# A first stage in a new order: norm rows spread by TensorE, low weight halves last, v statistics on ACT

## The chip, the cores and the metric

The kernel runs on one core of a Trainium2 chip. The metric is the device time of one execution in microseconds (us). It is 938.45 as the median of three runs of the kernel before (935.6 to 940.73).

## The reference, cut to what matters

One layer of a decoder trunk on 512 tokens of 1024 channels, in float32. The change touches the front of it: the first norm, the branch that computes v and u from the normed x, and the gating of the two.

```
x = layer_norm(x, ln_in_g, ln_in_b)                     # 512 x 1024
z = x @ w_in + b_in                                     # split into u_a, v_a, x_b, gate_b, q_c, merge
v = layer_norm(gelu(v_a), ln_v_g, ln_v_b)               # 512 x 1024
s = einsum('gts,bcsgd->bctgd', tril(w_s), v as chunks of 128 x 8 groups of 128) + b_s
o_a = gelu(u_a) * s                                     # branch A
...                                                     # branch B (recurrence), branch C (attention)
y = g_a * (o_a @ p_a) + g_b * (o_b @ p_b) + g_c * (o_c @ p_c)
x = layer_norm(ALPHA * x + y @ w_o + b_o, ...);  x = layer_norm(ALPHA * x + moe(x), ...)
```

## The kernel before, in words

All products of the trunk are made of three float32r products: each operand is split into a high part (a cast on ACT, line 82) and a low part (a subtraction on DVE, line 83), and TensorE adds hi x hi, hi x lo and lo x hi into one PSUM bank. `split` (lines 81 to 83) makes the two halves, `mm3` (lines 107 to 109) the three products.

The stages follow each other on TensorE: the v products, the u loop with the mixing of v (branch A), the merge of branch A with its gates, the attention branch with its merge, the recurrent branch with its gates, the output projection and the router, then sixteen experts in 18 blocks of tokens, and the last norm.

**The v stage** (lines 270 to 373) stands in a manual block: inside it every engine gets the instructions in the order in which they are written. x lies in four blocks of 128 tokens. For each block it takes the norm (statistics by two bn_stats, a reciprocal root by eight steps on one column, `rstd_ops`, then a centring and a scaling over 1024 columns), the transposes (`transx`, eight of 128x128 into two PSUM banks, each bank then split by two casts and two subtractions) and two products p(t, n) of 24 matmuls each, one for each half n of the 1024 v columns. Weights come as four raw tiles of 1 MB, two for each n. `split_w` makes both halves of a half tile at once. In `vmm` a product takes, for each half of the channels, hi x hi, lo x hi and hi x lo in turn. `vsplit` puts the transposes of the next block of x after the first eight matmuls of a product. `vout` adds the bias on DVE and takes the gelu on ACT, `vnorm` takes the statistics and the norm of v on DVE.

The two rows ln_in_g and ln_in_b come as DMAs that spread one row over 128 partitions (`bcast`, 512 KB each), issued on SP's queue behind the first block of x and ahead of the weights.

**Outside the manual block** a planner sets the order. It may put instructions of later code among those of the manual block where an engine has room: `residual` (lines 317 to 320, ALPHA x plus b_o, stored by POOL for later) and a chain on 10 columns for the recurrence (lines 539 to 554, with one exp on ACT) are written behind the block and run inside its time. The u loop (lines 384 to 406) is planned too: for each of eight groups g a product of 24 matmuls (`ztile`) gives u, eight short matmuls mix v with the lower triangle of w_s, two DVE steps gate them (lines 400 to 404), and a split writes the result. Each pair of groups has its own weights (`zunit`: a load into one of two raw buffers, two casts, two subtractions). The weights of the pairs after the first are issued only after the last norm of v (lines 385 to 388).

```
for d2 in range(4):
    with ExitStack() as after:
        for i in last if d2 else ():
            after.enter_context(tc.issue_after(i.ins))
        w = zunit(256)
    for c in range(2):
        ...
    residual(d2)
```

PSUM has eight banks: four for products (`mmps`) and four for transposes and the rest (`auxps`). SBUF tiles come from pools with a fixed number of buffers; a new tile waits for the last reader of the buffer that it takes over.

## Time and profile before

| | us |
|---|---|
| median of three runs | 938.45 |
| the profiled execution's own time | 938.02 |
| its span, first to last instruction | 936.3 |
| TensorE busy in it | 875.4 |
| DVE busy | 599.3 |
| ACT busy | 449.2 |
| mean granted TensorE clock | 0.983 |

The span is what the profiler saw of one execution; the execution's own time is a little longer. Every time in the rows further down counts from the start of that span. A busy TensorE is an engine with a matmul in flight, not one at its peak. In the timeline, the bracket behind a row is how long the engine stood idle before it and what ended the wait. The granted clock is 1.00 for 2.4 GHz and 0.50 for 1.2 GHz.

### The profile page before, as it was taken

Reading aid. Unit: us, or ns where it says so; the run is one execution under the profiler, and the core shown is the slowest. Engines: PE = TensorE matmul, PEld = TensorE weight load, DVE = VectorE, ACT = ScalarE, POOL = GpSimd, SP = SyncE. Lnnn points to the kernel's source line nnn. Section 1 sums busy time; section 2 is a strip of 40 time slices with the busy share of each in tenths; the row PEclk is TensorE's granted clock in tenths of the full one; section 3 lists DMA queues with packets and bytes.
Section 4 is the critical chain, followed back from the end, with each engine's and each line's share of the span. In section 5 each row is a group of like instructions: output and inputs, shape, how many; then the busy total and the mean of one; then the engine's idle time right before and its main releaser. Section 6 shows DMA issues by size and latency. Waiting matters only on the chain. (4 is left out here: it accounts for less than half of the span.)

```text
span 936.3 us, 11182 instructions
## 1 busy us (share of the span) xinstructions
PE 875.4 (93%) x4260; PEld 728.6 (78%) x4260; DVE 599.3 (64%) x1020; ACT 449.2 (48%) x628; POOL 90.5 (10%) x86
## 2 busy tenths in 40 slices
PE   3799999999999999999999999999987889999990
PEld 3587888889988888888878888788866778888870
DVE  6978555225555543345766865765288987689966
ACT  4324332224533442224777687533024666678851
POOL 0110000000000100000000000000001123232943
PEclk9999999999999999999999999999999999999995
DMA  8534222223233522212313322338573888799672
GB/s 339 203 113 157 91 90 90 90 90 135 91 97 128 184 90 90 90 57 102 99 69 124 135 74 84 94 121 345 231 275 116 285 308 288 234 311 388 175 170 102
DMA packets 29867, 148.89 MB, mean 159 GB/s; under 512 B 5537, under 2 KB 5793, under 8 KB 16496
## 3 DMA queue, kind: packets, MB, share of 16 engines
q1 hardware_dynamic: 21312, 128.81, 37.7%
q0 software_dynamic: 7056, 17.12, 7.0%
q10 hardware_dynamic: 1440, 2.19, 0.7%
q8 instruction: 35, 0.57, 0.2%
q14 instruction: 24, 0.20, 0.1%
HBM read 138.33 MB, written 18.35 MB: 167 GB/s over the span
## 5 line engine op out<-in xcount | busy, mean ns | idle before, releaser
L109 PE MATMUL mm<-hl 128*128 128x512 f32 x1440 | 333.8, 390 | 0.0
L109 PEld LDWEIGHTS mm<-hl 128*128 128x128 f32 x1440 | 269.1, 188 | 55.6 <-DVE lnr L126 0.2
L83 DVE TENSOR_TENSOR hl<-raw,hl 128x1024 fp32r<-128x1024 f32 (+1 forms) x121 | 142.4, 1183 | 135.4 <-ACT hl L82 134.9
L82 ACT CAST hl<-raw 128x1024 fp32r<-128x1024 f32 (+1 forms) x121 | 121.6, 1016 | 130.2 <-PE mm L109 118.1
L109 PE MATMUL mm<-o,hl 128*128 128x512 f32 x624 | 142.9, 389 | 1.1 <-ACT o L82 1.1
L109 PEld LDWEIGHTS mm<-o,hl 128*128 128x128 f32 x624 | 117.1, 188 | 25.8 <-ACT o L82 1.5
L109 PE MATMUL mm<-hl,xs 128*128 128x512 f32 x432 | 107.5, 404 | 1.1 <-DVE xs L83 1.1
L109 PEld LDWEIGHTS mm<-hl,xs 128*128 128x128 f32 x432 | 81.0, 191 | 20.3 <-DVE xs L83 1.9
L686 DVE TENSOR_TENSOR hl<-o,hl 128x1024 fp32r<-128x1024 f32 (+1 forms) x52 | 57.8, 1144 | 2.6 <-ACT hl L680 2.6
L1137 PE MATMUL mm<-hl,hT 128*128 128x512 f32 x196 | 50.6, 404 | 0.7 <-DVE hT L83 0.7
L680 ACT CAST hl<-o 128x1024 fp32r<-128x1024 f32 x48 | 48.1, 1052 | 1.7 <-PE mm L1137 1.7
L1137 PEld LDWEIGHTS mm<-hl,hT 128*128 128x128 f32 x196 | 35.6, 189 | 8.4 <-DVE hT L83 1.1
L1001 POOL DMA_INDIRECT xg<-x_d,ixg x1 | 1.1, 1092 | 402.3 <-DVE rtl L1060 402.3
L222 ACT ACTIVATE gate<-mm,col 128x512 f32<-128x512 f32 x24 | 16.5, 689 | 39.7 <-PE mm L109 39.6
L1126 DVE TENSOR_TENSOR hl<-raw,hl 128x1024 fp32r<-128x1024 f32 x26 | 30.7, 1223 | 4.5 <-ACT hl L1117 1.9
L1117 ACT CAST hl<-raw 128x1024 fp32r<-128x1024 f32 x32 | 31.9, 1052 | 0.0
L109 PE MATMUL mm<-memT,hl 128*128 128x256 f32 x192 | 27.3, 285 | 0.2 <-ACT memT L82 0.2
L300 PE MATMUL mm<-o,hl 128*128 128x512 f32 x96 | 25.1, 419 | 2.4 <-ACT o L82 2.4
L728 ACT COPY x1T<-aux 128x512 f32<-128x512 f32 x8 | 4.7, 587 | 44.0 <-PE aux L727 19.5
L109 PEld LDWEIGHTS mm<-memT,hl 128*128 128x128 f32 x192 | 24.9, 191 | 0.9 <-ACT memT L82 0.4
L300 PE MATMUL mm<-hl 128*128 128x512 f32 x96 | 25.1, 413 | 0.4 <-DVE hl L83 0.4
L300 PEld LDWEIGHTS mm<-o,hl 128*128 128x128 f32 x96 | 19.2, 204 | 7.3 <-ACT o L82 3.1
(319 smaller groups left out, 1140.9 us busy)
## 6 DMA issues: line engine op xcount, KB each, us to landing
raw<-in_wz_dram SPq DMA_DIRECT2D x32, 1024.0 KB, 4.8
o<-in_we_dram SPq DMA_DIRECT2D x24, 1024.0 KB, 7.4
raw<-in_we_dram SPq DMA_DIRECT2D x16, 1024.0 KB, 5.0
raw<-in_pac_dram SPq DMA_DIRECT2D x8, 1024.0 KB, 4.7
raw<-in_wkv_dram SPq DMA_DIRECT2D x8, 1024.0 KB, 4.9
rawx<-in_we_dram SPq DMA_DIRECT2D x8, 1024.0 KB, 5.9
raw<-in_pb_dram SPq DMA_DIRECT2D x4, 1024.0 KB
raw<-in_wo_dram SPq DMA_DIRECT2D x4, 1024.0 KB, 4.8
```

The lines of the kernel that those rows point to most:

```text
L82: act.copy(hi, src)
L83: dve.tensor_tensor(lo, src, hi.bitcast(F32), op=ALU.subtract)
L109: pe.matmul(ps, lhsT=a(sa_), rhs=b(sb_), start=first and i == 0, stop=last and i == 2)
L222: act.activation(store[j], ps, AF.Sigmoid, bias=cc(C_M + br_i * 8 + j))
L300: pe.matmul(ps, lhsT=xT(k, slice(t * P, (t + 1) * P))(sx), rhs=wv[2 * n + k // 4, k // 2 % 2][:, sw, k % 2, :], start=i == 0, stop=i == 23)
L680: act.copy(t[:, 0], raws[key, i // 2][:, (i % 2) * 1024:(i % 2 + 1) * 1024])
L686: (eng or dve).tensor_tensor(t[:, 1, c0:c1], src[:, c0:c1], t[:, 0, c0:c1].bitcast(F32), op=ALU.subtract)
L728: act.copy(x1T.rearrange("p k n -> p (k n)"), ps)
L1001: pool.indirect_dma_start(out=xg, out_offset=None, in_=x1_d[:, :], in_offset=bass.IndirectOffsetOnAxis(ap=ix[:, b:b + 1], axis=0), bounds_ ...
L1117: act.copy(dnh[key][:, :, n * 512:(n + 1) * 512], dn_half(key, n))
L1126: eng.tensor_tensor(dnl[key][n], dn_half(key, n), dnh[key][:, :, ns].bitcast(F32), op=ALU.subtract)
L1137: pe.matmul(ps, lhsT=hT[:, sa_, f, :], rhs=dn[sb_][:, f, :], start=i + f == 0, stop=i + f == 3)
```

## The change

In the front, all in one manual block that now begins ahead of the first DMA and ends behind the u loop:

- ln_in_g and ln_in_b come as one DMA of two rows (8 KB) into two partitions of the tile that later holds v. TensorE spreads them over 128 partitions with four fp32 matmuls (a column of the identity, repeated, times the rows) into four PSUM banks; two short matmuls on the identity stand ahead of them. x's first block reads its factors from these banks on DVE, and ACT copies them into SBUF for the other blocks.
- A raw weight tile is loaded in two DMAs each. b_s and b_o are loaded last.
- `split_w` becomes `w_hi` (ACT) and `w_lo` (DVE). A product p(t, n) first takes all its 16 hi x hi and lo x hi matmuls, then its 8 hi x lo (`V_KS`). For the first two blocks of x the first 16 of all four products run first, into four open banks, then the last 8 of all four. The low halves of the weights are made in between.
- The sums of x2 and x3 and their squares are taken on ACT (Copy and Square with an accumulator), and one root chain of ten steps serves both. The transposes of x2 and x3 stand ahead of a product and no longer inside one.
- The mean and the variance of v come from the gelu's accumulator and a Square on ACT, and ACT scales v (Identity with scale and bias).
- The two matmuls and eight DVE steps that prepare b_s stand before the last v product, as do the first u weights. The u loop is written out: a product, then the mixing and gating of the group before (`mix_mm` and `mix_ev`, which hold the lines of the old loop), and the residuals in turns 2 to 5.

Elsewhere: the chain on 10 columns is issued after the last exp of the attention; two pad tiles and a wider xb move addresses; the three buffers for gathered tokens are all slices of y (one had its own tile).

```diff
+    const.tile([P, 64], F32, name="pad")
...
+        gi = s0.tile([P, D], F32, name="gi")
+        bi = s0.tile([P, D], F32, name="bi")
+        v = yp.tile([P, NT, AW], F32, name="y")
+        man = ExitStack()
+        man.enter_context(tc.manual_schedule())
+        rw = v[0:2, NT - 1, :]
+        sp.dma_start(rw, rows[0:2, :])
         loadx(0, 2)
-        gi = bcast(sp, s0, "ln_in_g", "gi")
-        bi = bcast(sp, s0, "ln_in_b", "bi")
         raws = [load_w(op_, "o", 2), load_w(hlp, "hl", 2)]
         loadx(1)
-        raws += [load_w(rawp, "raw"), load_w(rawp, "raw")]
+        raws += [load_w(rawp, "raw", 2), load_w(rawp, "raw", 2)]
         loadx(2)
         loadx(3)
         sa = st_a.enter_context(tc.tile_pool(name="sa", bufs=1, reuse_waits="tile"))
-        v = yp.tile([P, NT, AW], F32, name="y")
-        man = ExitStack()
-        man.enter_context(tc.manual_schedule())
         bv = bcast(sp, sa, "b_v", "bv")
         sp.dma_start(col, cols)
-        bo = bcast(sp, s0, "b_o", "bo")
-        bs = bcast(sp, sa, "b_s", "bs")
         wst = sa.tile([P, 8, P], F32, name="wst")
         sp.dma_start(wst, ws)
+        bs = bcast(sp, sa, "b_s", "bs")
+        bo = bcast(sp, s0, "b_o", "bo")
         wv = {}
...
+        hv = [slice(n * 512, (n + 1) * 512) for n in range(2)]
+
+        def w_hi(i, h):
+            wv[i, h] = (op_ if i < 2 else hlp).tile([P, 2, 2, 512], F32R, name="o" if i < 2 else "hl")
+            act.copy(wv[i, h][:, 0], raws[i][:, 2 * h:2 * h + 2, :])
+
+        def w_lo(i, h):
+            t_ = wv[i, h]
+            dve.tensor_tensor(t_[:, 1], raws[i][:, 2 * h:2 * h + 2, :], t_[:, 0].bitcast(F32), op=ALU.subtract)
+
+        V_KS = [(4 * h + k, s, 0) for h in range(2) for s in range(2) for k in range(4)] + [(k, 0, 1) for k in range(8)]
         def vmm(t, n, ps, lo, hi):
-            ks = [(4 * h + k, sx, sw) for h in range(2) for sx, sw in ((0, 0), (1, 0), (0, 1)) for k in range(4)]
             for i in range(lo, hi):
-                k, sx, sw = ks[i]
+                k, sx, sw = V_KS[i]
                 pe.matmul(ps, lhsT=xT(k, slice(t * P, (t + 1) * P))(sx), rhs=wv[2 * n + k // 4, k // 2 % 2][:, sw, k % 2, :],
                           start=i == 0, stop=i == 23)
...
         def vfull(t, n):
             ps = mmps()
             vmm(t, n, ps, 0, 24)
             return ps
...
+        vst = s0.tile([P, NT, 4], F32, name="vst")
+        xst = s0.tile([P, 2, 3], F32, name="xst")
+        nmr = s0.tile([P, NT], F32, name="nmr")
+
+        def vout(t, n, ps):
+            vs = v[:, t, hv[n]]
+            dve.tensor_tensor(vs, ps, bv[:, hv[n]], op=ALU.add)
+            return act.activation(vs, vs, AF.Gelu_apprx_tanh, accum_out=vst[:, t, n:n + 1])
+
+        def vstat(t):
+            dve.tensor_scalar(vst[:, t, 2:3], vst[:, t, 0:1], vst[:, t, 1:2], -1.0 / AW, op0=ALU.add, op1=ALU.mult)
+            act.activation(v[:, NT - 1, :] if t < NT - 1 else gi, v[:, t, :], AF.Square, bias=vst[:, t, 2:3],
+                           accum_out=vst[:, t, 3:4])
+
+        def vnorm(t0, t1):
+            z, ops = rstd_ops(None, t1 - t0, vst[:, t0:t1, 3])
+            weave(ops)
+            dve.tensor_tensor(nmr[:, t0:t1], z, vst[:, t0:t1, 2], op=ALU.mult)
+            for t in range(t0, t1):
+                i_ = act.activation(v[:, t, :], v[:, t, :], AF.Identity, scale=z[:, t - t0:t - t0 + 1], bias=nmr[:, t:t + 1])
+            return i_
+
...
-        mv = ln_stats(xts_[0])
+        ps = auxps()
+        for i in range(2):
+            pe.matmul(ps[:, :P], lhsT=ident, rhs=ident, start=True, stop=True)
+        bc = {}
+        for i in range(2):
+            for n in range(2):
+                bc[i, n] = mmps()
+                pe.matmul(bc[i, n], lhsT=ident[0:2, i:i + 1].to_broadcast([2, P]), rhs=rw[:, hv[n]], start=True, stop=True)
+        x0 = xts_[0]
+        x0q = [(slice(c * 256, (c + 1) * 256), slice(c % 2 * 256, (c % 2 + 1) * 256), c // 2) for c in range(4)]
+        mv = ln_stats(x0)
         rstd, ops = rstd_ops(mv)
...
+        for n in range(2):
+            act.copy(gi[:, hv[n]], bc[0, n])
+        weave(ops, [lambda c=c, d=d, n=n: dve.scalar_tensor_tensor(x0[:, c], x0[:, c], mv[:, 0:1], bc[0, n][:, d],
+                                                                   op0=ALU.subtract, op1=ALU.mult) for c, d, n in x0q])
+        act.copy(bi[:, hv[0]], bc[1, 0])
+        w_hi(0, 0)
+        act.copy(bi[:, hv[1]], bc[1, 1])
+        w_hi(0, 1)
+        for c, d, n in x0q:
+            dve.scalar_tensor_tensor(x0[:, c], x0[:, c], rstd, bc[1, n][:, d], op0=ALU.mult, op1=ALU.add)
         transx(0)
-        split_w(0, 1)
-        split_w(1, 0)
-        split_w(1, 1)
-        p00 = vfull(0, 0)
+        w_hi(1, 0)
+        w_hi(1, 1)
+        p00 = mmps()
+        vmm(0, 0, p00, 0, 16)
         layer_norm(xts_[1], xts_[1], gi, bi)
-        split_w(2, 0)
-        split_w(2, 1)
-        split_w(3, 0)
-        split_w(3, 1)
-        p01 = vsplit(0, 1, 1)
+        for i in (2, 3):
+            for h in range(2):
+                w_hi(i, h)
+        p01 = mmps()
+        vmm(0, 1, p01, 0, 16)
+        w_lo(0, 0)
+        w_lo(0, 1)
+        transx(1)
+        w_lo(1, 0)
+        w_lo(1, 1)
+        p10, p11 = mmps(), mmps()
+        vmm(1, 0, p10, 0, 16)
+        for i in range(2):
+            act.activation(v[:, NT - 2, :], xts_[2 + i], AF.Copy, accum_out=xst[:, i, 0:1])
+        w_lo(2, 0)
+        for i in range(2):
+            dve.tensor_scalar(xst[:, i, 1:2], xst[:, i, 0:1], -1.0 / D, None, op0=ALU.mult)
+            act.activation(v[:, NT - 2, :], xts_[2 + i], AF.Square, bias=xst[:, i, 1:2], accum_out=xst[:, i, 2:3])
+        w_lo(2, 1)
+        w_lo(3, 0)
+        w_lo(3, 1)
+        vmm(1, 1, p11, 0, 16)
+        vmm(0, 0, p00, 16, 24)
+        vmm(1, 0, p10, 16, 24)
+        vmm(0, 1, p01, 16, 24)
+        vmm(1, 1, p11, 16, 24)
         pool.affine_select(wst, wst, pattern=[[0, 8], [1, P]], compare_op=ALU.is_ge, fill=0.0,
                            base=0, channel_multiplier=-1)
+
+        def xnorm(i, f=None):
+            xr = xts_[2 + i]
+            c = lambda: dve.scalar_tensor_tensor(xr, xr, xst[:, i, 1:2], gi, op0=ALU.add, op1=ALU.mult)
+            c()
+            dve.scalar_tensor_tensor(xr, xr, zx[:, i:i + 1], bi, op0=ALU.mult, op1=ALU.add)
+
+        zx, ops = rstd_ops(None, 2, xst[:, :, 2])
+        weave(ops)
+        xnorm(0)
         vout(0, 0, p00)
-        ln = ln_begin(xts_[2], xts_[2], gi)
+        transx(2)
+        p20 = vfull(2, 0)
+        vout(1, 0, p10)
         vout(0, 1, p01)
-        p10 = vfull(1, 0)
-        ln_end(xts_[2], ln, bi)
-        p11 = vsplit(1, 1, 2)
-        vout(1, 0, p10)
-        ln = ln_begin(xts_[3], xts_[3], gi)
+        vstat(0)
         vout(1, 1, p11)
-        p20 = vfull(2, 0)
-        ln_end(xts_[3], ln, bi)
-        p21 = vsplit(2, 1, 3)
-        vnorm(0)
+        vstat(1)
+        xnorm(1)
+        p21 = vfull(2, 1)
+        transx(3)
         vout(2, 0, p20)
+        vnorm(0, 2)
         p30 = vfull(3, 0)
-        vout(2, 1, p21)
-        vnorm(1)
-        p31 = vfull(3, 1)
-        vout(3, 0, p30)
-        vnorm(2)
-        last = [vout(3, 1, p31), vnorm(NT - 1)]
-        man.close()
-        oa = o_tiles()
...
-        for d2 in range(4):
-            with ExitStack() as after:
-                for i in last if d2 else ():
-                    after.enter_context(tc.issue_after(i.ins))
-                w = zunit(256)
...
+        raw_u = {}
+
+        def load_u(d2):
+            raw_u[d2] = load_raw(wz[wz_next[0]].rearrange("p (k n) -> p k n", n=256), 8, 256)
+            wz_next[0] += 1
+
+        load_u(0)
+        load_u(1)
+        wu_ = {0: split_raw(raw_u[0], 8, 256, lambda i: op_.tile([P, 2, 1024], F32R, name="o") if i
+                            else hlp.tile([P, 2, 1024], F32R, name="hl"))}
+        vout(2, 1, p21)
+        vstat(2)
+        vnorm(2, 3)
+        p31 = vfull(3, 1)
+        vout(3, 0, p30)
+        vout(3, 1, p31)
+        vstat(3)
+        vnorm(3, 4)
+        oa = o_tiles()
+        us = {}
+
+        def u_mm(g):
+            ps = mmps()
+            ztile(ps, wu_[g // 2], g % 2)
+            us[g] = sa.tile([P, T], F32, name="u", bufs=2)
+            act.activation(us[g], ps, AF.Gelu_apprx_tanh, bias=cc(C_U + g))
+
...
+        for g in range(8):
+            if g % 2 == 0 and g < 6:
+                wu_[g // 2 + 1] = split_raw(raw_u[g // 2 + 1], 8, 256)
+                if g // 2 + 2 < 4:
+                    load_u(g // 2 + 2)
+            u_mm(g)
+            if g:
+                mix_ev(g - 1, mix_mm(g - 1))
+            if 2 <= g < 6:
+                residual(g - 2)
+        mix_ev(7, mix_mm(7))
+        man.close()
...
+    with tc.issue_after(exp_i.ins):
...
-            xb = sb.tile([P, 2, T + 3], F32, name="xb")
+            xb = sb.tile([P, 2, T + 64], F32, name="xb")[:, :, :T + 3]
...
+    rt.tile([P, 104], F32, name="pad")
...
-    xgs = [mo.tile([P, D], F32, name="xg0")] + [xg_[:, i, :] for i in range(2)]
+    xgs = [xg_[:, i, :] for i in range(3)]
```

## Rows read from the trace of the kernel before

**Rows 1.** The page, part 1: engine, busy us (share), instructions.
```profile
PE 875.4 (93%) x4260; PEld 728.6 (78%) x4260; DVE 599.3 (64%) x1020; ACT 449.2 (48%) x628; POOL 90.5 (10%) x86
```

**Rows 2.** By stretch: busy us of each engine (instructions), clock, DMA share, GB/s.
```profile
125.43:690.00 564.57, 562.13 (x2750) 473.02 (x2749) 301.75 (x416) 254.45 (x346) 3.07 (x5) 1.00 0.34 121
```

**Rows 3.** TensorE's timeline: start, us, instructions [idle before <-what ended it].
```profile
11.78 1.94 PE L187 MATMUL aux<-ident,x 128*128 128x128 f32 x8 [11.78 <-DVE x L338]
...
16.94 6.99 PE L300 MATMUL mm<-o,hl 128*128 128x512 f32 x22 [2.36 <-ACT o L82]
...
26.10 1.09 PE L187 MATMUL aux<-ident,x 128*128 128x128 f32 x8 [0.35 <-DVE x L158]
...
43.67 1.18 PE L187 MATMUL aux<-ident,x 128*128 128x128 f32 x8 [4.48 <-DVE lt L549]
44.50 5.46 PE L300 MATMUL mm<-hl 128*128 128x512 f32 x16
49.80 5.60 PE L300 MATMUL mm<-o,hl 128*128 128x512 f32 x24
...
72.46 1.88 PE L378 MATMUL aux<-wst,ones 128*128 128x512 f32 x4
...
118.28 1.05 PE L397 MATMUL aux<-wst,y 128*128 128x128 f32 x8
...
124.62 1.05 PE L397 MATMUL aux<-wst,y 128*128 128x128 f32 x8
```

**Rows 4.** Table by stretch, behind the hole at 39 to 44 us.
```profile
44.50:47.60 3.10, 3.10 (x10) 2.47 (x8) 2.95 (x10) 1.23 (x4) 0.53 (x1) 0.50 0.02 5
```

**Rows 5.** DVE's timeline of the front.
```profile
3.88 1.29 DVE L114 BATCH_NORM_STATS2 bnst<-x 128x6 f32<-128x512 f32 x2 [3.88 <-DMA x<-in_x_dram]
...
8.51 0.48 DVE L335 SCALAR_TENSOR_TENSOR x<-x,bnmv,gi 128x256 f32<-128x256 f32 x1 [2.91 <-DMA gi<-in_rows_dram]
...
11.20 1.67 DVE L338 SCALAR_TENSOR_TENSOR x<-x,lnr,bi 128x256 f32<-128x256 f32 x4
...
20.33 1.28 DVE L114 BATCH_NORM_STATS2 bnst<-x 128x6 f32<-128x512 f32 x2
...
23.09 0.15 DVE L124 TENSOR_SCALAR lnv<-bnmv 128x1 f32<-128x1 f32 x1
...
24.76 1.28 DVE L158 SCALAR_TENSOR_TENSOR x<-x,lnr,bi 128x1024 f32<-128x1024 f32 x1
```

**Rows 6.** ACT's timeline of the front.
```profile
11.04 1.05 ACT L82 CAST o<-o 128x1024 fp32r<-128x1024 f32 x1 [8.95 <-DMA o<-in_wz_dram]
...
36.30 0.63 ACT L306 ACTIVATE y<-y 128x512 f32<-128x512 f32 x1 [1.87 <-DVE y L305]
...
37.89 1.28 ACT L542 ACT_TABLE_LOAD   x1
```

**Rows 7.** The same by stretch, 4 to 8 us.
```profile
4.00:6.00 2.00, 0.00 (x0) 0.00 (x0) 1.53 (x4) 0.00 (x0) 0.00 (x0) 1.00 0.58 212
6.00:8.00 2.00, 0.00 (x0) 0.00 (x0) 0.00 (x0) 0.00 (x0) 0.00 (x0) 1.00 0.95 299
```

**Rows 8.** DVE's groups, 0 to 73 us: busy us, mean ns, idle.
```profile
L83 DVE TENSOR_TENSOR hl<-raw,hl 128x1024 fp32r<-128x1024 f32 x6 | 7.0, 1217 | 0.0
L83 DVE TENSOR_TENSOR hl<-aux,hl 128x256 fp32r<-128x256 f32 x16 | 6.4, 420 | 4.8 <-ACT hl L82 4.8
L319 DVE SCALAR_TENSOR_TENSOR x<-x,bo 128x1024 f32<-128x1024 f32 x4 | 6.4, 1588 | 0.0
...
L305 DVE TENSOR_TENSOR y<-mm,bv 128x512 f32<-128x512 f32 x7 | 4.7, 681 | 0.0
```

**Rows 9.** Waits, 0 to 50 us: total us, times, longest.
```profile
ACT hl L82 <- DVE hl L83: 8.2, 6, 3.8
```

**Rows 10.** ACT's timeline near the end of the kernel.
```profile
906.05 1.15 ACT L1371 ACTIVATE yb<-y,ln2s 128x1024 f32<-128x1024 f32 x1 [4.06 <-DVE ln2s L1370]
```

**Rows 11.** The page, part 6: DMA issues, KB each, us to landing.
```profile
raw<-in_wz_dram SPq DMA_DIRECT2D x32, 1024.0 KB, 4.8
```

More of the change, by code (lines that the diff above doesn't have):

```diff
@@ L323, in transx @@
             transpose_split(xts_[t], dsth(t, 0), dsth(t, 1))
-        def vsplit(t, n, next_t):
-            ps = mmps()
-            vmm(t, n, ps, 0, 8)
-            transx(next_t)
-            vmm(t, n, ps, 8, 24)
-            return ps
-        mv = ln_stats(xts_[0])
-        rstd, ops = rstd_ops(mv)
-        x0h = [slice(c * 256, (c + 1) * 256) for c in range(4)]
-        weave(ops, [lambda c=c: dve.scalar_tensor_tensor(xts_[0][:, c], xts_[0][:, c], mv[:, 0:1], gi[:, c],
-                                                         op0=ALU.subtract, op1=ALU.mult) for c in x0h])
@@ L337, in trunk @@
-        for c in x0h:
-            dve.scalar_tensor_tensor(xts_[0][:, c], xts_[0][:, c], rstd, bi[:, c], op0=ALU.mult, op1=ALU.add)
-        split_w(0, 0)
+        ps = auxps()
[6 more added lines that the diff above has]
+                pe.matmul(bc[i, n], lhsT=ident[0:2, i:i + 1].to_broadcast([2, P]), rhs=rw[:, hv[n]], start=True, stop=True)
@@ new lines, in trunk, with mix_mm @@
+        vout(3, 1, p31)
[8 more added lines that the diff above has]
+            act.activation(us[g], ps, AF.Gelu_apprx_tanh, bias=cc(C_U + g))
+        def mix_mm(g):
+            pv = auxps()
+            for ch in range(NT):
+                pe.matmul(pv[:, ch * P:(ch + 1) * P], lhsT=v[:, ch, g * P:(g + 1) * P],
+                          rhs=wst[:, g, :], start=True, stop=True)
+            return pv
@@ new lines, in mix_ev @@
+        def mix_ev(g, pv):
+            s = sa.tile([P, T], F32, name="s", bufs=2)
+            dve.scalar_tensor_tensor(s.rearrange("p (c t) -> p c t", t=P),
+                                     pv.rearrange("p (c t) -> p c t", t=P), cc(C_VG + g),
+                                     bs[:, None, g * P:(g + 1) * P].to_broadcast([P, NT, P]),
+                                     op0=ALU.mult, op1=ALU.add)
+            dve.tensor_tensor(s, s, us[g], op=ALU.mult)
+            split(oa(0, g), oa(1, g), s)
```

64 lines of the change are left out of this document (17 added, 47 removed).

## The prediction

> **What bounds the kernel now.** I read four views, in this order. The page's engine line comes first: TensorE is busy for 875 of 936 us [rows 1], so time is won only where TensorE stands still or runs at its lower clock level. The table by stretch comes next: from the u loop's end at 125.43 us to 690 us TensorE is busy 562.1 of 564.6 us [rows 2]. What the front loses is therefore never given back later, and what it gains should arrive at the end undiminished. Third is TensorE's timeline of the front [rows 3]. The reader is to see four losses there. The first transpose starts at 11.78. Two matmuls later there is a hole of 2.36, and the 22 matmuls behind it need 6.99. In steady flow 24 need 5.60, of which 0.39 is the last one's own length, so 0.227 each; 22 would need 5.16, and 1.8 is lost. Then there is a hole of 4.48 ahead of the transposes of the third x block. Behind that hole 16 matmuls need 5.46 in place of 3.79, because the granted clock is 0.50 from 44.5 to 47.6 [rows 4], the lower of the two levels, after the engine had stood still. Fourth come DVE and ACT. DVE works without a break through that hole: what TensorE waits for is a row of DVE work (weight halves, four norms, two residuals, a chain on 10 columns) in which the norm of x2 stands late. In front of everything, DVE waits 2.91 for gi, a 128-partition spread by DMA [rows 5], and ACT waits until 11.04 for the first weight [rows 6].
>
> **The change, step by step.** I lay the new order out engine by engine with the durations of the trace. All times below are us from the start of the profiled execution.
>
> *Start of x0.* One 8 KB DMA stands ahead of x0 on SP in place of two 512 KB spreads behind it. x0 is issued one issue later (0.43), at about 4.3 in place of 3.88 for its arrival. Before, x0's norm ended at 12.87 with 2.91 of that waiting for gi [rows 5]. Without the wait and with 0.43 more it ends at 10.4, and its first half allows transposes from 9.3 in place of 11.78. The spread costs four fp32 matmuls of 512 columns on TensorE. The trace has two such, on the ones column: four records, 1.88 with the drain, so about 0.86 each at full clock [rows 3], and at the lower level twice that. The rows come no later than x0 did, 3.88. Upper end: four at 1.7 from there would end at 10.7 and push x0's second half back by about 1.5. Lower end: 3.4, ended by 7. I take an end near 8.5, between the two, and so no cost on the path.
>
> *First weights.* The two spreads moved about 1.05 MB between 4 and 8, when DMA carried 212 and 299 GB/s [rows 7]. That is about 4.1 us, and less the 0.43 it brings every later load about 3.6 forward: the first weight half from 11.04 to about 7.5. Ends: 11.5 (nothing won, 0.43 lost) and 6.9. I take 7.5, the value that the bytes give. The last of the eight halves then lands near 17.3. ACT in its new order: cast (0,0) from 7.5, copy of a bi half 0.6 (a gelu of that size takes 0.63), cast (0,1), then x0's four casts in turn with DVE's four subtractions (0.42 each, [rows 8]; about 2.5 in all) until 12.6, then six weight casts of 1.0 [rows 6] until 18.6. TensorE runs behind ACT here: hi products of p00 and p01 end 6 matmuls after the last cast, at 20.0.
>
> One dependency in this is easily missed. Before, ACT's second cast from a PSUM bank starts only when DVE's subtraction from the same bank has ended (six waits, 8.2 us, [rows 9]). So DVE's second half of x0, which reads bi from PSUM, stands behind ACT's copy of the same bank, and that copy stands in ACT's queue behind weight cast (0,0), hence behind the first weight's arrival: 7.5 + 1.05 + 0.6 = 9.15, before DVE's 9.6 for that step. At an arrival of 11.5 it would be 13.2, so this edge makes a late weight cost twice. The Trainium skill, PSUM — Partial Sum Buffer, section "PSUM bank collisions raise a hardware error", says that two engines may not touch one bank and quadrant at once, two reads included. The trace's six waits agree. By that rule the result is the sum with the late arrival, the first rival below.
>
> *Four open banks.* x1's transposes 0.9 (eight in 0.8 plus their drain, [rows 3]) to 20.9. p10 must run in step with x1's casts and subtractions, 16 matmuls in about 4.5 instead of 3.6, to 25.4; p11's hi half 3.6 to 29.0; the 32 low products of all four 7.25 to 36.3. DVE must keep up: x0's last subtraction 13.1, x1's norm 5.6 (20.33 to 26.0, [rows 5]) 18.7, two low halves at 1.17 to 21.0, x1's subtractions to 23.6, six more low halves and two tiny steps to 31.0 (needed at 32.6), the root chain for two blocks (10 steps of about 0.2, by the 8 steps from 23.09 to 24.76) 33.0, centre and scale of x2 2.5 to 35.5, needed at 36.3. The margin is 0.8. What made room on DVE is gone from this stretch: x2's and x3's statistics (1.3 each) to ACT, four residuals (6.4, [rows 8]) to the u loop, the 10-column chain with its table loads on ACT (1.28 each, [rows 6]) behind the last exp. Before, the four banks were full at 49.8; the gain here is 13.5.
>
> *Second half of v.* x2's transposes now stand ahead of p20 and x3's ahead of p30, not inside a product, and each costs TensorE 0.9 and a wait of about 0.5 for the first casts. So 36.3 + 1.4 + 48 × 0.227 = 48.6; + 1.4 + 5.4 = 55.4 for p30; the two ones matmuls 1.7; p31 5.4: 62.6. Here new waits stand on DVE: each vstat step waits for the gelu and its accumulator read on ACT (a 128x1024 square took 1.15 and a short read, [rows 10]). Behind the first two is the norm of x3: vout, gelu and square in turn bring it to about 46.4, needed at 48.6. Behind the third and fourth are the last vouts and the final v norm: p31 62.6, vout 0.7, gelu 0.65, square 1.2, root chain 1.7, ACT scaling 1.1 and hand-overs give about 68.7 to 71.5, with the wait for ACT's earlier work. The first mixing product comes behind two u products, at 62.6 + 10.9 = 73.5. If that cover were gone, the price is the overrun itself.
>
> *u loop.* Eight turns of 6.34 (118.28 to 124.62, [rows 3]) give 113.3 in place of 125.43. Per turn DVE has three steps of 512 columns (2.1, by the 0.68 of one in [rows 8]), a weight half (1.2) and in four turns a residual (1.6). ACT has at most two weight casts and two steps of 0.63, 3.4. Both fit. The residuals' DMAs on POOL's queue have hundreds of us before they are read. A raw buffer is refilled behind its split: landing 4.8 [rows 11], two casts 2.1, one subtraction 1.2, so 8.1 of the 12.7 that two turns give.
>
> *The rest.* The pads, the wider xb and xg in y add no instruction, and before the first gather TensorE's reads of y are over. They are worth 0, with ±1 as bound since the planner lays the later code out anew. The 10-column chain of some 20 steps (3 to 4 us of DVE) behind the last exp lies beside gate products on TensorE; its bounds are 0 and 1.
>
> *Sum.* 125.43 − 113.3 = 12.1 earlier, and by [rows 2] this stays. The profiled execution took 938.02 (span 936.3), 0.4 under the median 938.45 of the three runs. 938.02 − 12.1 = **926**. Its own range is 922 to 930: down to 922 if every transpose wait vanishes and weights land at 6.9; up to 930 if the spread runs at the lower level and the planner's layout costs 1, with some 1.5 of hand-overs that I did not count.
>
> **Rivals.** *Late, thin start.* If the weights land as late as before, ACT's chain ends near 22.2, everything to 36.3 moves by 3.6, and with TensorE standing in pieces the clock may fall to the lower level as at 44.5, 1.7 a time. The gain is then 12.1 − 3.6 − 1.7 or less: 931 to 934. For it: ACT is the engine that TensorE follows there, and ACT waits for the load first of all. Against it: 1 MB less stands ahead. *The gain is given back at the hand-over.* The merge behind the manual block needs its first gate weights split when the last mixing product ends. If the planner places these behind the eighth turn's evaluation, TensorE waits about 5 and restarts at the lower level, 1.7: 932.5. Against it: before, code from behind the manual block was woven into it (residuals and the 10-column chain amid the norms). *Nothing moves*, the middle being laid out anew so that it loses about what the front wins: 936 to 940; [rows 2] speaks against it. *Slower.* The u loop is in written order, so ACT's queue stops at a weight cast whose load has not landed, and with it the gelu that frees TensorE's bank. It decides if a refill takes over 12.7 instead of 8.1. Three refills that each miss by 6 or more would lose 18 against the 12.1 won: 944 or more. For it: nothing of a later pair can pass; against it: a refill would have to take more than twice what the rows say.
>
> **Numbers.** Forecast 0.68, late start 0.13, hand-over 0.08, nothing 0.05, slower 0.06. About 0.5% (4.7 us) is what a measurement of this kernel can tell from no change. Faster by more 0.88, within 0.06, slower 0.06. The range goes from 920, a little under the forecast's own end for a middle laid out better, to 934, the end of the first two rivals.
>
> **What would show it.** First transposes near 9.5, p01's hi part ended near 20, the four banks full near 36, no hole above 1.5 between 20 and 113 and a clock of 1.00 there, first mixing product near 73.5, the u loop over near 113. A TensorE hole at 20 to 36 released by DVE would show the margin of 0.8 wrong; one released by a weight's DMA the late start; a hole behind the last mixing product the hand-over.

## The result, and the profile after

| | before | after |
|---|---|---|
| median of five runs | 939.83 (935.60 to 941.66) | 928.44 (924.31 to 929.88) |
| profiled execution, its own time | 938.02 | 924.31 |
| its span | 936.3 | 922.6 |
| mean granted TensorE clock in it | 0.983 | 0.985 |

Over all executions on record, seven of after and five of before, the ratio of the means is 0.9874, with a 95% interval of 0.9845 to 0.9904: the kernel became faster by 9 to 14.6 us. 926.0 was predicted, with a range of 920 to 934. The profiled execution of after is the fastest of its five, 4.1 below their median; so the profiles are 13.7 apart where the medians are 11.4 apart.

The page of after, part 1, against [rows 1]: TensorE is busy 2.7 us longer in a span 13.7 shorter. The four spread matmuls (7.19), the two short ones on the identity (1.22) and the slow ones behind them are added; what went is idle time.

```profile
PE 878.1 (95%) x4272; PEld 729.4 (79%) x4272; DVE 586.4 (64%) x995; ACT 462.5 (50%) x658; POOL 91.2 (10%) x86
```

TensorE's timeline of after (start, us, instructions, and in brackets the idle time before them with its releaser) stands against [rows 3]. The reader is to see that no hole above 0.43 is left between 11.95 and 115.43, and that the four banks are full (the first four products p00, p01, p10 and p11 have all their matmuls) at 37.53, 12.3 earlier than before.

```profile
2.79 7.19 PE L352 MATMUL mm<-y,ident 2*128 2x512 f32 x8
9.91 1.11 PE L188 MATMUL aux<-ident,x 128*128 128x128 f32 x4
11.18 1.12 PE L188 MATMUL aux<-ident,x 128*128 128x128 f32 x4
11.95 3.67 PE L307 MATMUL mm<-o,hl 128*128 128x512 f32 x10
15.82 1.65 PE L307 MATMUL mm<-o,hl 128*128 128x512 f32 x6 [0.21 <-ACT o L296]
17.32 3.96 PE L307 MATMUL mm<-hl 128*128 128x512 f32 x16
21.12 1.04 PE L188 MATMUL aux<-ident,x 128*128 128x128 f32 x8
22.18 0.73 PE L307 MATMUL mm<-o,hl 128*128 128x512 f32 x2
23.34 3.47 PE L307 MATMUL mm<-o,hl 128*128 128x512 f32 x14 [0.43 <-ACT hl L82]
...
37.53 1.03 PE L188 MATMUL aux<-ident,x 128*128 128x128 f32 x8
38.59 6.15 PE L307 MATMUL mm<-o,hl 128*128 128x512 f32 x24
...
64.27 2.88 PE L109 MATMUL mm<-hl 128*128 128x512 f32 x12
...
75.15 1.05 PE L463 MATMUL aux<-wst,y 128*128 128x128 f32 x8
75.96 0.71 PE L109 MATMUL mm<-hl 128*128 128x512 f32 x2
76.84 5.32 PE L109 MATMUL mm<-hl 128*128 128x512 f32 x22 [0.17 <-DVE hl L83]
82.00 1.05 PE L463 MATMUL aux<-wst,y 128*128 128x128 f32 x8
...
113.73 1.95 PE L463 MATMUL aux<-wst,y 128*128 128x128 f32 x16
115.43 22.02 PE L109 MATMUL mm<-hl 128*128 128x512 f32 x96
```

The table by stretch tells where the 13.7 us of the two spans come from. Columns: from and to; length; busy us and instructions of PE, PEld, DVE, ACT, POOL; granted clock, DMA share, GB/s. The stretches run from the last mixing matmul to the output projection, through the router, through the experts, and to the end. First before:

```profile
125.43:656.70 531.27, 528.83 (x2573) 444.75 (x2572) 287.27 (x381) 247.20 (x334) 3.07 (x5) 1.00 0.33 114
656.70:727.50 70.80, 61.08 (x356) 52.00 (x354) 48.90 (x179) 19.45 (x30) 3.63 (x4) 0.98 0.54 203
727.50:911.90 184.40, 179.35 (x854) 145.74 (x853) 153.39 (x225) 131.88 (x197) 66.60 (x50) 0.99 0.83 272
```

Then after:

```profile
115.43:646.00 530.57, 528.20 (x2573) 444.79 (x2572) 290.56 (x401) 246.78 (x335) 3.06 (x5) 1.00 0.33 115
646.00:716.80 70.80, 61.01 (x355) 51.99 (x353) 48.78 (x179) 19.38 (x30) 3.51 (x4) 0.98 0.55 206
716.80:898.30 181.50, 176.11 (x853) 145.44 (x853) 153.07 (x225) 131.96 (x197) 67.66 (x50) 0.99 0.83 275
```

The front is 10.0 shorter (125.43 to 115.43), the middle 0.7, the router 0.0, the experts 2.9 with the same number of instructions, the end 0.1. So two things are to be explained: why the front gave 10.0 and not 12.1, and why the experts, which the change hardly touches, became shorter.

One thing limits all comparisons below. In the profiles of all kernels the router's stretch took between 69.5 and 74.5, with no order in it that follows the edits. So effects of 2 us are read from the stage's own stretch in the profile, not from medians. The stages' own stretches repeat better: three kernels with the front of before ended it at 125.43, 124.56 and 124.76, and three with the front of after at 115.43, 115.48 and 115.72. An effect on the front below 1 us is thus shown only where a row shows its wait.

### The profile page after: what moved, and what is told of

Read it like the earlier page. It is cut to its first block, busy times and chain, and to the rows that moved or that the text cites. A ratio compares the mean times of both kernels' runs of the same rounds, so it can differ in the third digit from the quotient of the medians.

```text
span 922.6 us, 11201 instructions
## 1 busy us (share of the span) xinstructions
PE 878.1 (95%) x4272; PEld 729.4 (79%) x4272; DVE 586.4 (64%) x995; ACT 462.5 (50%) x658; POOL 91.2 (10%) x86
## 4 chain that ended last, share of the span: by engine, by line
PE 74%; DVE 11%; DMA 5%; ACT 4%; POOL 3%; issue 2%; SPq 0%; POOLq 0%; ACTq 0%; DVEq 0%
PE mm L109 60%; PE aux L109 4%; PE mm L307 3%; PE mm L1221 3%; DVE hl L768 2%; POOL rawx L1255 2%; DMA y<-acc_d 1%; DMA o<-in_we_dram 1%; DMA x<-in_x_dram 1%; DMA col<-in_cols_dram 1%; PE aux L1163 1%; DVE hl L83 1%; PE aux L463 1%; DMA acc_d<-yb,ix_x 1%; ACT hl L82 1%
## 5 line engine op out<-in xcount | busy, mean ns | idle before, releaser
L109 PE MATMUL mm<-hl 128*128 128x512 f32 x1416 | 327.7, 390 | 0.2 <-DVE hl L83 0.2
L109 PEld LDWEIGHTS mm<-hl 128*128 128x128 f32 x1416 | 264.6, 188 | 54.7 <-DVE hl L83 0.6
L83 DVE TENSOR_TENSOR hl<-raw,hl 128x1024 fp32r<-128x1024 f32 (+1 forms) x116 | 136.2, 1181 | 136.4 <-ACT hl L82 135.8
L82 ACT CAST hl<-raw 128x1024 fp32r<-128x1024 f32 (+1 forms) x116 | 116.3, 1014 | 126.1 <-PE mm L109 113.7
L109 PEld LDWEIGHTS mm<-o,hl 128*128 128x128 f32 x624 | 117.1, 188 | 25.9 <-ACT o L82 1.6
L109 PE MATMUL mm<-hl,xs 128*128 128x512 f32 x432 | 105.1, 399 | 1.1 <-DVE xs L83 1.1
L1085 POOL DMA_INDIRECT y<-x_d,ixg x3 | 3.2, 1058 | 402.7 <-DVE rtl L1144 402.1
L1085 POOL DMA_INDIRECT y<-x_d,ix_x x13 | 17.8, 1370 | 70.7 <-PE aux L1163 67.4
L109 PE MATMUL mm<-hl,yh 128*128 128x512 f32 x96 | 24.6, 400 | 0.0
```

What stands on the lines that cost most here:

```text
L82: act.copy(hi, src)
L83: dve.tensor_tensor(lo, src, hi.bitcast(F32), op=ALU.subtract)
L109: pe.matmul(ps, lhsT=a(sa_), rhs=b(sb_), start=first and i == 0, stop=last and i == 2)
L1085: pool.indirect_dma_start(out=xg, out_offset=None, in_=x1_d[:, :], in_offset=bass.IndirectOffsetOnAxis(ap=ix[:, b:b + 1], axis=0), bounds_ ...
```

## The experiments

The front is measured as the time of the last mixing matmul (125.4 before, 115.4 after); the experts' stretch as above (184.4 and 181.5). Times are medians of the runs beside the kernel before on the same chip; the ratio behind them, with its 95% interval, is estimated from all these runs and need not be the quotient of the two medians.

**What the order is worth.** After, but with the low halves right behind the high ones, and each product's 24 matmuls in one piece:

```diff
-        w_hi(1, 0)
-        w_hi(1, 1)
+        w_lo(0, 0)
+        w_lo(0, 1)
+        for h in range(2):
+            w_hi(1, h)
+            w_lo(1, h)
         p00 = mmps()
-        vmm(0, 0, p00, 0, 16)
+        vmm(0, 0, p00, 0, 24)
...
```

> The changed kernel with the low weight halves made right behind the high ones and each of the first four v products run through in one (24 matmuls), as before; all else as in the change. DVE has the same work in another order. Theory A (low halves last is what lets TensorE run while DVE is short): p00 waits for low halves until about 19, x1's norm ends near 24.6, p01 near 30, the four banks are full near 42 in place of 37.5; 932 to 934. Theory B (DVE's sum of work sets the end in any order): four banks full within 1 us of 37.5; 928 to 929.

937.33 against 938.66: ratio 0.9977 (0.9955 to 0.9998). The front took 126.0. Nearly the whole gain is gone, though the spread, the statistics on ACT and the hoisted work stay as in after. TensorE's timeline of this kernel, with the row of its stretch table from 24.33 to 34.57:

```profile
20.01 1.98 PE L307 MATMUL mm<-hl 128*128 128x512 f32 x8
28.35 6.97 PE L307 MATMUL mm<-hl 128*128 128x512 f32 x16 [6.36 <-DVE hl L300]
35.16 1.03 PE L188 MATMUL aux<-ident,x 128*128 128x128 f32 x8
```
```profile
24.33:34.57 10.24, 6.22 (x14) 4.52 (x15) 7.16 (x11) 0.00 (x0) 0.47 (x1) 0.50 0.41 155
```

The hole of 6.36 stands before p01: DVE does the norm of x1 ahead of the low halves. The 16 matmuls behind it need 6.97 in place of 3.79 at the lower level. So theory A held, but with the four banks full at 47.66 the delay is 10.1 where 4.5 was expected. Part of it is an accident: a step of the 10-column chain, which the planner put there, held DVE for 2.08 until its load had landed.

```profile
18.80 1.28 DVE L114 BATCH_NORM_STATS2 bnst<-x 128x6 f32<-128x512 f32 x2
22.16 0.17 DVE L614 TENSOR_SCALAR lt<-col 128x10 f32<-128x10 f32 x1 [2.08 <-DMA col<-in_cols_dram]
```

So the order over four open banks is worth 10.6 of the front here, or about 8.5 if these 2.08 are taken off.

**What the hoisted work is worth.** Before, but with residuals and the 10-column chain kept out of the front:

```diff
-            residual(d2)
+            with tc.issue_after(last[1].ins):
+                residual(d2)
...
+    with tc.issue_after(exp_i.ins):
+        lam = col[:, C_LAM ...
```

> The kernel before, with the planner kept from putting the four residuals ahead of the last v norm and most of the 10-column chain ahead of the last exp. DVE loses some 6 us of work ahead of the norm of x2, and TensorE's order stays as it was. Theory A (a good part of the gain is only that this work left the front): the hole of 4.48 at 39 us and the low clock behind it (1.7) vanish, 5 to 6 us are won, 933 to 935. Theory B (the hole stands because DVE is short anyway, and only the new order of products fills it): the hole shrinks to 2 to 3 and less than 3 us are won, 937 to 939.

936.89 against 938.66: 0.9971 (0.995 to 0.9991). The hole before x2's transposes shrank from 4.48 [rows 3] to 2.31, and the clock still fell to 0.50 behind it:

```profile
41.69 1.94 PE L187 MATMUL aux<-ident,x 128*128 128x128 f32 x8 [2.31 <-DVE x L158]
43.28 4.68 PE L300 MATMUL mm<-hl 128*128 128x512 f32 x16
```

The front took 123.3. In the old order the hoisted work cost 2.2, by which the hole shrank; what remains of the hole is the row of DVE work that the front itself needs.

**What the spread by TensorE is worth.** After, with gi and bi by DMA as before:

```diff
-        sp.dma_start(rw, rows[0:2, :])
         loadx(0, 2)
+        gi = bcast(sp, s0, "ln_in_g", "gi")
+        bi = bcast(sp, s0, "ln_in_b", "bi")
...
```

> The changed kernel, with ln_in_g and ln_in_b spread by DMA as before, and without the TensorE spread, its copies and the two short matmuls on the identity. Theory A (by the prediction's sum): first weight back near 11, ACT's chain of casts about 2 to 3 us later, TensorE's clock low until some 3.6 us after its first steady work, the four banks full near 40 to 41 in place of 37.5; 931 to 933. Theory B (DVE's chain and not ACT's sets the four banks, so the late start is swallowed): four banks full within 1 us of 37.5, 928 to 929.

927.7 against 938.66: 0.988 (0.9855 to 0.9906), not to be told from the change itself. First transposes 11.16, four banks full 39.36, front 117.2. So the spread is worth 1.8, less than the 2.5 to 3.5 expected. ACT's first weight cast shows why:

```profile
10.62 1.05 ACT L294 CAST o<-o 128x1024 fp32r<-128x1024 f32 x1 [8.53 <-DMA o<-in_wz_dram]
```

With the spread by DMA it waits for its load until 10.62. In after the same load lands at 8.0 (issued at 2.11, 5.9 to landing), 2.6 earlier, but the cast begins at 8.79, since ACT's copies of the spread stand ahead of it. The 1.83 between the two casts is found again in the four banks (1.83) and at the end of the front (1.8). The first recorded rise of the clock was expected 3.6 behind TensorE's first work and came 4.5 behind it, at 15.62.

**Why the spread took 7.2.** After, with the same eight matmul records over 128 rows, of which 126 are cleared to zero:

```diff
-        rw = v[0:2, NT - 1, :]
-        sp.dma_start(rw, rows[0:2, :])
+        rw = v[:, NT - 1, :]
+        dve.memset(rw, 0.0)
+        sp.dma_start(rw[0:2, :], rows[0:2, :])
...
-                pe.matmul(bc[i, n], lhsT=ident[0:2, i:i + 1].to_broadcast([2, P]), rhs=rw[:, hv[n]], start=True, stop=True)
+                pe.matmul(bc[i, n], lhsT=ident[:, i:i + 1].to_broadcast([P, P]), rhs=rw[:, hv[n]], start=True, stop=True)
```

> The changed kernel with the spread of ln_in_g and ln_in_b made over 128 rows (the other 126 rows are cleared and add nothing) and not over 2. The four matmuls move as many columns, and the DMA of the two rows goes out behind the clearing, some 0.4 us later. In the change TensorE ran without a break from 2.8 to 10.0 us and its clock rose only at 13.5. Theory A (matmuls over two rows don't count as work for the clock): the clock rises during the spread, by about 7 us, the spread ends near 8.5 and x0's first transposes start near 9.3 at full clock; the u loop ends 1 to 2 us earlier. Theory B (the clock rises at a time that has nothing to do with the rows): 13 to 14 us as before, and the front is 0 to 0.5 us later.

926.84 against 939.90: 0.9857 (0.9836 to 0.9878). The first recorded rise of the clock is at 7.74; in after it is at 13.49 and with DMA spread at 15.6. The spread's row on TensorE, and two rows by stretch:

```profile
3.84 5.61 PE L353 MATMUL mm<-y,ident 128*128 128x512 f32 x8 [0.99 <-DMA y<-in_rows_dram]
```
```profile
3.84:7.74 3.90, 3.90 (x5) 1.82 (x6) 2.22 (x7) 0.70 (x2) 0.00 (x0) 1.00 0.92 298
7.74:9.45 1.71, 1.71 (x4) 0.38 (x2) 1.64 (x8) 1.06 (x2) 0.00 (x0) 1.00 0.96 278
```

One record needs about 0.85 ahead of 7.74 and 0.43 behind it, although the clock column prints 1.00 for both: ahead of the first recorded rise the level is to be read from the durations. So matmuls of 2 rows ran from 2.79 to 9.98 without a break and TensorE stayed at the lower level; matmuls of 128 rows were followed by the higher level. The other profiles agree: in all six kernels with the 2-row spread the first recorded rise stands between 13.26 and 15.21, in the two with the 128-row spread at 7.74 and 8.99. The spread's length fell from 7.2 to 5.6. So theory A held for the clock, but its gain did not arrive, since the memset held the rows' DMA back (issued at 2.03 in place of 0.81) and every load behind it: first transposes 10.35, four banks full 39.51, front 117.4. What is late is mostly the weights. Four of ACT's casts now wait for their loads, the first until 9.74 and the last until 20.18; it ends at 21.2 in place of 19.6.

```profile
20.18 1.05 ACT L297 CAST hl<-raw 128x1024 fp32r<-128x1024 f32 x1 [0.20 <-DMA raw<-in_wz_dram]
```

**An attempt at a better version.** The 128-row spread with the rows' DMA behind x0's, and x3's transposes four matmuls before p21's end:

```diff
-        rw = v[0:2, NT - 1, :]
-        sp.dma_start(rw, rows[0:2, :])
+        rw = v[:, NT - 1, :]
+        dve.memset(rw, 0.0)
         loadx(0, 2)
+        sp.dma_start(rw[0:2, :], rows[0:2, :])
...
-        p21 = vfull(2, 1)
+        p21 = mmps()
+        vmm(2, 1, p21, 0, 20)
         transx(3)
+        vmm(2, 1, p21, 20, 24)
...
```

> The changed kernel with three things that the runs point to: the spread over 128 cleared rows, the two rows' DMA issued behind x0's two (so that the clearing delays neither x0 nor much else), and x3's transposes put after 20 of the 24 matmuls of p21 and no longer behind it. Theory A: x0 lands at 3.9, the clock is up by 7 to 8 us, x0's first transposes start near 9.3, the four banks are full near 36.3, the wait of 0.5 ahead of p30 goes, and the u loop ends at 113.3 to 114 in place of 115.4; 926 to 927, no more than the timing can tell. Theory B (ACT's chain behind the first weight sets the start, and the clock is no part of it): 115 to 116, no gain.

926.98 against 940.09: 0.9864 (0.9837 to 0.989). Expectation missed: the rows landed later, the spread began at 5.40 and the first transposes stood at 11.71. The wait before p30 did go (its 24 matmuls need 5.60, not 6.15), but the front is 116.8. It is no better than the change. The clock rose at 8.99 here and the first weight had landed at 6.5, yet ACT's first weight cast began only at 10.52, behind the copies of the late spread. So what sets the start is ACT's queue, as theory B has it, though not with its number. Some 0.7 more is a step of the 10-column chain, which held DVE for 1.07 at 23.59 in place of 0.17.

**Statistics of x on DVE.** After, with x2's and x3's sums and squares back from ACT:

```diff
-            act.activation(v[:, NT - 2, :], xts_[2 + i], AF.Copy, accum_out=xst[:, i, 0:1])
...
+        xmv = [ln_stats(xts_[2 + i]) for i in range(2)]
...
```

> The changed kernel with the statistics of x2 and x3 taken on DVE (bn_stats) behind the low weight halves, not on ACT. DVE gets 3.4 us more ahead of the norm of x2, which in the change was ready 1.3 us before TensorE wanted it. Theory A (DVE's chain is just inside TensorE's): the transposes of x2 start 2 us later, with a hole of 2 us before them, and the front ends 2 us later. Theory B (there is more cover than that): within 0.5 us.

928.02 against 939.90: 0.9877 (0.9851 to 0.9903). Front 118.0. TensorE's timeline shows the hole where DVE had been relieved:

```profile
39.38 1.06 PE L188 MATMUL aux<-ident,x 128*128 128x128 f32 x8 [1.77 <-DVE x L405]
```

In after DVE ended that norm at 36.24, 1.3 before TensorE asked for it:

```profile
34.95 1.29 DVE L406 SCALAR_TENSOR_TENSOR x<-x,lnr,bi 128x1024 f32<-128x1024 f32 x1
```

Here it ended at 39.23. The 3.0 that the statistics cost DVE used up the 1.3 and left 1.77 of hole; with the waits behind it the step is worth 2.6 of the front, as theory A has it.

**Statistics of v on DVE:**

```diff
-            return act.activation(vs, vs, AF.Gelu_apprx_tanh, accum_out=vst[:, t, n:n + 1])
+            return act.activation(vs, vs, AF.Gelu_apprx_tanh)
...
+                mv = ln_stats(v[:, t, :])
...
```

> The changed kernel with the statistics and the norm of v on DVE as before. DVE gets about 8 us more between 42 and 75 us, where it stood idle for over 15. Theory A (v's statistics are off the path on either engine): the u loop ends within 0.7 of 115.4; 927 to 930. Theory B (the last v norm is late for the first mixing product, or the gelu waits behind it): 1.5 us or more later, with a hole before the first mixing product at 75.

928.15 against 940.09: 0.9886 (0.9854 to 0.9918). Front 116.1, 0.7 later, by short holes (0.41 the first) at the start of the u products. The step is nearly off the path.

**The order alone.** DMA spread and both statistics on DVE, so of the change only the order, the hoisted work, the raw loads in halves and the pads stay (the edits of three experiments above together).

> The changed kernel with the rows spread by DMA and all statistics back on DVE (x2, x3 and v): what is left of the front is the order, high halves first over four banks, and the written-out u loop. Theory A (the parts add): 1.8 us for the spread and 2.6 for x's statistics as measured one by one, and 0 to 1 for v's, so the u loop ends at 119.8 to 121 in place of 115.4; 930 to 932. Theory B (without relief for DVE the order doesn't hold, and a hole of over 3 us with the low clock behind it comes back): 123 or later; 935 or more.

930.31 against 940.09: 0.9903 (0.9879 to 0.9927). Front 121.55, a little over what was expected:

```profile
41.70 1.42 PE L188 MATMUL aux<-ident,x 128*128 128x128 f32 x8 [2.39 <-DVE x L387]
43.13 6.90 PE L305 MATMUL mm<-o,hl 128*128 128x512 f32 x24
```

The hole is back, and with it the lower level (42.27 to 45.68). The order needs the room that the statistics make on DVE. Without spread and statistics 3.9 of the front are won, and 2.2 of them the old order also won when the hoisted work left it; the new order adds some 1.7. With spread and statistics on ACT the same order is worth 8.5 to 10.6, as the first experiment shows. These two need each other. The spread and the two statistics among themselves nearly add up: 1.8, 2.6 and 0.7 one by one make 5.1, and together they are worth 6.1.

**The layout alone.** Before, with the pads, the wider xb and xg in y:

```diff
+    const.tile([P, 64], F32, name="pad")
...
-            xb = sb.tile([P, 2, T + 3], F32, name="xb")
+            xb = sb.tile([P, 2, T + 64], F32, name="xb")[:, :, :T + 3]
...
+    rt.tile([P, 104], F32, name="pad")
...
-    xgs = [mo.tile([P, D], F32, name="xg0")] + [xg_[:, i, :] for i in range(2)]
+    xgs = [xg_[:, i, :] for i in range(3)]
```

> The kernel before with the address part of the change alone: the two pads, the wider xb, all three gather buffers in y. In the profiles the experts' stretch (760 to 912 us of the kernel before) was 2.8 us shorter after the change, spread evenly over its matmuls, and no instruction of it was changed. Theory A (chance of one execution, or the start that shifts it): this kernel takes as long as the one before, 938 to 941, and its expert stretch stays within 1 us of before. Theory B (addresses make these matmuls faster): 935 to 938, and the stretch is 2 to 3 us shorter.

936.55 against 938.66: 0.9982 (0.9961 to 1.0002). In the time alone this can't be told from nothing. The profile tells it: the experts' stretch is 181.2, with the front at 124.6, so theory B holds. The groups of TensorE from 560 to 905 (busy us, mean ns of one, idle) of this kernel:

```profile
L109 PE MATMUL mm<-hl,xs 128*128 128x512 f32 x432 | 105.0, 399 | 0.8 <-DVE xs L83 0.8
...
L1140 PE MATMUL mm<-hl,hT 128*128 128x512 f32 x196 | 49.8, 399 | 0.8 <-DVE hT L83 0.8
```

and of before:

```profile
L109 PE MATMUL mm<-hl,xs 128*128 128x512 f32 x432 | 107.5, 404 | 1.1 <-DVE xs L83 1.1
...
L1137 PE MATMUL mm<-hl,hT 128*128 128x512 f32 x196 | 50.6, 404 | 0.7 <-DVE hT L83 0.7
```

The same matmuls of the same shape are each some ns shorter. The distance from start to start says it more plainly (median over the records): 227 and 229 ns here and in after, 234 and 235 before. 7 ns on 432 and 6 on 196 are 4.2 us, of which 3.2 show in the stretch. The weight loads of both groups keep their 188 ns. What differs is where tiles start in a partition, read from the built programs. xs, the operand that is loaded as weights here (hT, that of the second group, lies 10,240 bytes behind it in all of them), starts at byte 207,200 before, which is 32 past a multiple of 64, and in after at 203,776, a multiple of 512; the expert weights, which stream through, moved from 256 past a multiple of 512 onto one.

**Another pad, before's order:** xg in y and a pad of 32 bytes, so that xs starts at 203,136 (a multiple of 64 and 128, 384 past one of 512).

```diff
+    rt.tile([P, 8], F32, name="pad")
...
```

> The kernel before with all gather buffers in y and one pad of 32 bytes a partition ahead of the experts' tiles, so that xs and hT (what TensorE loads as weights there) start at a multiple of 64 bytes and no longer 32 past one. The front is that of before. Theory A (the start address makes each of these matmuls 7 ns shorter): start to start 227 in place of 234 ns, and the stretch from 760 to 912 us of the kernel before is 2.5 to 3 us shorter; 935 to 937. Theory B (what matters is the larger shift, or where the gather lands): 234 ns as before, 938 to 939.

937.49 against 939.90: 0.9975 (0.9956 to 0.9995). 232 ns for both groups, experts 183.0: between the two cases, so a multiple of 128 is not enough.

**After with a pad of 448 in place of 416 bytes**, xs at 203,808 (32 past a multiple of 512):

```diff
-    rt.tile([P, 104], F32, name="pad")
+    rt.tile([P, 112], F32, name="pad")
```

> The changed kernel with the experts' pad 32 bytes longer (448 in place of 416), so that xs and hT start 32 past a multiple of 64 bytes again; all else as in the change. Theory A (start address): the experts' matmuls go back to 234 ns start to start, the front keeps its 10 us; 2.5 to 3 us longer than the change, 930 to 932. Theory B: 227 ns, as the change.

927.3 against 939.90: 0.9863 (0.9837 to 0.9888). 235 and 233 ns, experts 183.4, front unchanged at 115.5. The groups:

```profile
L109 PE MATMUL mm<-hl,xs 128*128 128x512 f32 x432 | 107.2, 404 | 0.7 <-DVE xs L83 0.7
...
L1221 PE MATMUL mm<-hl,hT 128*128 128x512 f32 x196 | 50.3, 402 | 0.7 <-DVE hT L83 0.7
```

32 bytes of pad bring the old durations back. They move xs, hT and the other tiles allocated behind the pad, and not the expert weights. All fourteen profiles agree: in the nine with xs on a multiple of 512 xs' matmuls follow each other every 227 ns and the experts' stretch takes about 181 to 182, in the five others every 232 to 235 and 183 to 185. That the start addresses set the durations is shown; that the median falls with them is not, since 927.3 lies below after's 928.44.

**After with a pad of 288 bytes:** xs 384 past a multiple of 512, the weights' tiles on multiples of 512.

```diff
-    rt.tile([P, 104], F32, name="pad")
+    rt.tile([P, 72], F32, name="pad")
```

> The changed kernel with the experts' pad 128 bytes shorter, so that xs and hT start 384 past a multiple of 512 bytes (as in the run with the 32-byte pad, which gave 232 ns) while the weights' own tiles stay at multiples of 512. Theory A (any multiple of 64 or 128 bytes will do, and the 232 came from the weights' tiles at 256 past): 227 to 229 ns. Theory B (the start has to be a multiple of more than 128 bytes): 232 ns.

930.05, one run. 232 ns for both, experts 183.6, as with the pad of 32. So the weights' starts don't explain the 232; xs' own start does. Whether a multiple of 256 would do for xs stays open.

## Why the prediction was right, and which sizes were off

The mechanism held: the front shrank by the order over four open banks with DVE relieved, and the gain stayed to the end. That the total came within 2.4 us is in part luck. In the profiled pair the front gave 2.1 less than the 12.1 predicted and the rest 3.7 more. Between the medians the gain is 11.4, but 926 was counted down from an execution of 938.02, 1.8 under before's median; where the other executions of after lose their 4 us against the profiled one, no profile shows.

*Start of x0 and first weights.* x's first half landed at 4.23 (4.3 predicted). The term that failed is the spread: "I take an end near 8.5", with 10.7 as upper end. It ended at 9.98, because TensorE stayed at the lower level all through it and until 13.49. ACT's timeline shows how this got on the path; it did so through ACT's queue, not only by DVE's second half of x0 as written:

```profile
6.61 0.58 ACT L358 COPY gi<-mm 128x512 f32<-128x512 f32 x1 [1.12 <-PE mm L352]
8.31 0.58 ACT L361 COPY bi<-mm 128x512 f32<-128x512 f32 x1 [1.12 <-PE mm L352]
8.79 1.05 ACT L296 CAST o<-o 128x1024 fp32r<-128x1024 f32 x1
10.02 0.59 ACT L363 COPY bi<-mm 128x512 f32<-128x512 f32 x1 [0.18 <-PE mm L352]
10.50 1.05 ACT L296 CAST o<-o 128x1024 fp32r<-128x1024 f32 x1
...
13.78 2.00 ACT L296 CAST o<-hl 128x1024 fp32r<-128x1024 f32 x2
15.67 3.90 ACT L296 CAST hl<-raw 128x1024 fp32r<-128x1024 f32 x4
```

The copies wait for the spread's matmuls, and the weight casts stand behind the copies: first cast 8.79 (7.5), second 10.50 (9.15), the six others from 13.78 (12.6). The first weight half was mis-sized too: it landed at 8.0, so of the 1.29 by which the first cast is late 0.5 is the load and 0.79 the copies. No cast stood waiting for a load, so the late-start rival fell, but its price came in small by another way: p01's high part ended at 21.1 in place of 20.0. Behind the spread the lower level cost nothing more: in the run with the 448-byte pad the rise came only at 15.21, and p01's high part ended at 21.1 there too, since TensorE follows ACT. The bank edge named in the prediction is there, with its length:

```profile
10.64 0.87 DVE L366 SCALAR_TENSOR_TENSOR x<-x,lnr,mm 128x256 f32<-128x256 f32 x2 [0.63 <-ACT bi L363]
```

*Four open banks.* From 21.1 to 37.53 are 16.4 (16.3 predicted). DVE's x2 norm ended at 36.24, a margin of 1.3 (0.8). This is the step that carries the gain, and taking the order away confirmed it.

*Second half of v.* 26.7 in place of 26.3 up to the first u product: the wait behind each pair of transposes was about 0.55, as predicted, and p31 had one more behind the ones matmuls (6.05). One estimate was wrong without cost: the last v norm was to end by 68.7 to 71.5 and ended at 74.59, 0.56 before the first mixing matmul. ACT works through blocks 2 and 3 in order, so the root chain on DVE holds it twice:

```profile
67.40 1.25 ACT L334 ACTIVATE y<-y,nmr,lnr 128x1024 f32<-128x1024 f32 x1 [1.96 <-DVE nmr L332]
68.55 0.62 ACT L322 ACTIVATE y<-y 128x512 f32<-128x512 f32 x1
...
73.34 1.25 ACT L334 ACTIVATE y<-y,nmr,lnr 128x1024 f32<-128x1024 f32 x1 [1.95 <-DVE nmr L332]
```

The cover of two u products was used up but for that 0.56.

*u loop.* Its first turn needs 6.85 in place of 6.34, with a short hole for a weight's low half; the others run as predicted. The merge begins directly behind the last mixing matmul, so the hand-over rival fell. No refill was late, so the slower one fell too. Together 1.1 + 0.1 + 0.4 + 0.5 = 2.1 that the front lacks.

*The rest.* "They are worth 0, with ±1 as bound" is the other mis-sized term: the pads and xg in y were worth about 3 in the experts' stretch. The prediction looked for instructions added, and found none; it did not ask whether the same matmul takes as long from another start address. Why the middle became 0.7 shorter stays open. The 10-column chain behind the exp cost nothing visible there. Three of its DVE steps (0.5 together) still ran in the front; two of them, at 22.30 and 22.39, stand right ahead of the subtraction at 22.46 that ACT and then TensorE wait for, so some 0.2 of the hole of 0.43 is theirs.

*A reading without weight.* Up to the hole at 39 us of the kernel before, DVE had done three norms (x0, x1 and x2), not four.

## What to carry to other kernels

When the engine that makes the second halves of split operands is the short one, let TensorE first do the products that need only the first halves, over as many open banks as there are, and free that engine at the same time: here the order won some 1.7 of the front without that relief, and 8.5 or more with it. A matmul that is cheap at full clock must be priced at the lower level in the first microseconds (the spread took 7.2, where its price at full clock was 3.4), and whoever queues behind its result must be counted with it. When tiles move in SBUF, compare the start-to-start distance of long rows of equal matmuls before and after: 32 bytes were worth some 2 us here, on the experts alone.

## What had not been expected of the hardware

- Start address of a matmul's stationary operand (xs): 128x512 float32r matmuls follow each other every 227 ns with it on a multiple of 512 bytes, every 232 at 384 past one, every 234 to 235 at 32 past a multiple of 64, though the recorded weight load has 188 ns each time. Why, no run shows.
- Matmuls over 2 rows, unbroken from 2.79 to 9.98, left TensorE at the lower level until 13.49, when 128-row work had begun at 9.91 (13.26 to 15.21 in six kernels with this spread); with 128-row matmuls from 3.84 the rise came at 7.74, and from 5.40 at 8.99.
- The recorded clock starts with the first change: ahead of it 1.00 is printed while a 512-column record takes 0.85 in place of 0.43.
